# Half of the output gate's row in the differential mixer, gate transfers on GpSimd's queue, and seams in a new order, in a fused hybrid layer

## The chip, the cores and the metric

The kernel runs on one core of a Trainium2 chip. Five engines work beside each other, each with a queue of its own that it goes through in order: TensorE (PE in the profile, its weight loads PEld), VectorE (DVE), ScalarE (ACT), GpSimd (POOL) and SyncE (SP), which here only issues transfers. The metric is the device time of one execution in microseconds, the median of several runs.

## What is computed

One layer of a hybrid model on 512 positions of 2048 channels, and a norm behind it. All of it is fp32.

```python
mod = silu(c) @ w_ada + b_ada                     # 3 x 2048: shift, scale, gate
u = rms_norm(x, norm_w) * (1 + scale) + shift
proj = u @ w_in                                   # q, k, v, z of mixers A, B, C and the gates g_a, g_b, g_c
o_a = diff_attention(a_q, a_k, a_v, lam)          # 8 heads, two softmax maps each, one minus lam times the other
o_b = retention(b_q, b_k, b_v)                    # 8 heads, decaying scores, rotated q and k
o_c = dilated_mixture(c_q, c_k, c_v)              # 3 groups of 8 heads, windows of 1, 2 and 4 steps
y_m = (o_m * silu(m_z)) @ w_proj_m                # for m in a, b, c
merged = sigmoid(g_a) * y_a + sigmoid(g_b) * y_b + sigmoid(g_c) * y_c
h = x + gate * (merged @ w_out)
out = rms_norm(h, final_norm_w)
```

`gate`, the last third of `mod`, is a row of 2048 numbers (call it the output's gate; `gate phase` below means the merging of one mixer).

## The kernel before

Activations lie transposed, channels on the 128 partitions and the 512 positions along the free dimension. Every fp32 operand of a product is split into a high and a low part in a type that TensorE takes (`uh`, `ul` for the layer's input u; `wh`, `wl` for weights; `yh`, `yl` for a mixer's gated output), and `mm3` (L174) multiplies high by high, low by high and high by low into the same accumulator. A weight tile is loaded as `wr` by SyncE (1024 x 128, 512 KB), ScalarE casts it to `wh`, VectorE subtracts `wl`. There are three buffers of each. A projection of 128 columns takes two such tiles and 48 products. Accumulators are the eight banks of PSUM: two called `pj`, six called `at`. Nearly all instructions are recorded by one helper, so their line is L86 and they are told apart by their tiles.

The work goes in stages: projections in a form that saves products (up to some 1370 us, untouched by the change); mixer C; its gate phase; mixer A; its gate phase; mixer B; its gate phase; the output.

- **Mixer C** (the loop over heads behind L1073) keeps its order as written (`pinned`). A head makes its third key and z by four half projections (`half_step`, 24 products each), between which the scores of three groups stand. Queries and keys of the first two groups come from DRAM (`ql`, `kc`, `r`), `band` and `tri4` are masks.
- **Mixer A** (`a_scores`, `a_turn`, `a_values`, `rms_gate`): each of 8 heads projects Q, K and Z. In the middle of each projection (`mid`) the former head's leftover work is placed: transposing its scores e0 to e3, its values, its norm (square root on ScalarE, a reciprocal of 128 x 512 on VectorE), and then this head's scores.
- **Mixer B** (`rotate`, `b_scores`, `b_values`): four pairs of heads, Q and K rotated with `cos` and `sin`, two Z.
- **`gate_phase`** (L770) multiplies `y` by `w_proj` in 16 tiles (db), four or six of which start ahead of the mixer's last output. `gate_cols` loads the gate tile `gsg` (two buffers), `close` multiplies the accumulator by it, adds the sum so far (`gpr`, one buffer, from `part` in DRAM) and stores it back to `part` from ScalarE's queue. In the last phase the sum is split to `mh`, `ml`.
- **Output**: `merged @ w_out` in five column groups, `n`; four accumulators (one for each 128 positions), the products of a group going tile by tile (`t`, 24 products each). `gate_part` takes 256 rows and 512 columns of `w_ada`, weighs each row with `silu(c)` and sums them on VectorE into `gacc` (32 loads `gwa` of 512 KB in all, 64 operations), two parts in each tile of the first group and one in each after; `gate_sum` adds over the partitions by a product with ones. `residual` multiplies by the gate and adds to `hx`.

A scheduler places the instructions of mixers A and B, the gate phases and the output by a model of their durations and then keeps each engine's order; C and the stages ahead are pinned. So what a line in the source moves is seen only in the engines' order.

## Time and profile before

| what | us |
|---|---|
| median of 3 runs (2648.42 to 2651.3) | 2649.44 |
| the profiled execution | 2653.55 |
| its span, first to last instruction | 2651.8 |
| TensorE busy | 2543.9 |
| VectorE busy | 1919.4 |
| ScalarE busy | 1132.2 |
| GpSimd busy | 290.5 |

The profile shows one execution. Busy time counts an engine's instructions, a transfer's issue not among them. TensorE is busy for 96% of the span, so the seams between stages are read in a table of stretches: the width of a stretch less PE's busy time is what TensorE stood still, and the granted clock below 1.00 means that some of its products ran at 1.2 instead of 2.4 GHz. A wait is put down to what came last. The rows stand in a section of their own below.

### The profile page before, as it was taken

The page shows a single profiled execution, that of the slowest core. Times are in us where ns is not written, and L with a number is a line of the kernel's source. Part 1 is how long each engine was busy: PE and PEld are TensorE (multiplying, and loading weights), DVE is VectorE, ACT ScalarE, POOL GpSimd, SP SyncE. Part 2 cuts the span into 40 slices and gives each one's busy share as a digit, 9 for nine tenths or more (in the row PEclk, how much of TensorE's full clock was granted, in tenths as well). Part 3 has the DMA queues.
Part 4 walks back from the last instruction along what each step waited for, and adds up shares of the span by engine and source line. Part 5 has one row for each costly group of instructions (what it writes and reads, how often), then busy time and mean ns, then how long its engine had stood idle before and what let it go on. Part 6 is the DMA issues. An engine that isn't in the chain of part 4 may idle for free. (4 is left out here: it accounts for less than half of the span.)

```text
span 2651.8 us, 36979 instructions
## 1 busy us (share of the span) xinstructions
PE 2543.9 (96%) x14539; PEld 2231.4 (84%) x14539; DVE 1919.4 (72%) x2646; ACT 1132.2 (43%) x1461; POOL 290.5 (11%) x336
## 2 busy tenths in 40 slices
PE   6989999999999999999999999999999989999898
PEld 5777778999999999998878888788888768878678
DVE  7994888777787777877786776357767456776664
ACT  4224433443443333333336665346656145643122
POOL 2342001221122221212000000000000000000000
PEclk9999999999999999999999999999999999999999
DMA  9776666766666666676665554643233663337862
GB/s 343 253 272 227 233 206 232 235 209 204 225 221 220 225 216 214 220 232 220 222 200 152 159 149 133 191 124 88 83 93 87 189 183 106 89 106 216 303 210 104
DMA packets 386082, 503.26 MB, mean 190 GB/s; under 512 B 18898, under 2 KB 250084, under 8 KB 384756
## 3 DMA queue, kind: packets, MB, share of 16 engines
q1 hardware_dynamic: 364340, 448.83, 52.9%
q0 software_dynamic: 10048, 35.23, 3.8%
q10 hardware_dynamic: 11520, 16.85, 1.7%
q8 instruction: 114, 1.87, 0.3%
q14 instruction: 60, 0.49, 0.1%
HBM read 449.33 MB, written 51.51 MB: 189 GB/s over the span
## 5 line engine op out<-in xcount | busy, mean ns | idle before, releaser
L86 ACT CAST xh<-xr 128x2048 fp32r<-128x2048 f32 x196 | 374.2, 1909 | 584.7 <-PE at L86 494.3
L86 DVE TENSOR_TENSOR xl<-xr,xh 128x2048 fp32r<-128x2048 f32 x196 | 451.2, 2302 | 195.5 <-ACT xh L86 193.9
L86 ACT CAST wh<-wr 128x1024 fp32r<-128x1024 f32 (+2 forms) x275 | 240.2, 890 | 324.0 <-PE at L86 102.4
L86 PE MATMUL pj<-uh,wl 128*128 128x512 f32 x944 | 370.8, 393 | 5.9 <-DVE wl L86 3.3
L86 PE MATMUL pj<-uh,wh 128*128 128x512 f32 x944 | 373.6, 396 | 2.9 <-ACT wh L86 2.3
L86 PE MATMUL pj<-ul,wh 128*128 128x512 f32 x944 | 369.6, 392 | 0.0
L86 DVE TENSOR_TENSOR wl<-wr,wh 128x1024 fp32r<-128x1024 f32 (+2 forms) x241 | 240.9, 1013 | 142.2 <-ACT wh L86 141.3
L86 DVE TENSOR_TENSOR xr<-xr 128x512 f32<-128x512 f32 x448 | 329.1, 735 | 18.0 <-DMA xr<-in_w_in_dram 6.7
L86 PE MATMUL at<-fh,xl 128*128 128x256 f32 x864 | 246.2, 285 | 4.5 <-DVE xl L86 4.4
L86 PE MATMUL at<-fl,xh 128*128 128x256 f32 x864 | 245.3, 284 | 0.0
L86 PE MATMUL at<-fh,xh 128*128 128x256 f32 x864 | 245.2, 284 | 0.0
L86 PEld LDWEIGHTS pj<-uh,wl 128*128 128x128 f32 x944 | 178.1, 189 | 44.7 <-DVE wl L86 4.5
L86 PEld LDWEIGHTS pj<-uh,wh 128*128 128x128 f32 x944 | 178.6, 189 | 38.1 <-ACT wh L86 2.7
L86 PEld LDWEIGHTS pj<-ul,wh 128*128 128x128 f32 x944 | 178.6, 189 | 35.1
L86 PEld LDWEIGHTS at<-fh,xl 128*128 128x128 f32 x864 | 166.6, 193 | 5.9 <-DVE xl L86 5.5
L86 PEld LDWEIGHTS at<-fh,xh 128*128 128x128 f32 x864 | 166.6, 193 | 0.0
L86 PEld LDWEIGHTS at<-fl,xh 128*128 128x128 f32 x864 | 166.6, 193 | 0.0
L86 PE MATMUL at<-uh,xl 128*128 128x256 f32 x576 | 163.1, 283 | 0.0
L86 PE MATMUL at<-ul,xh 128*128 128x256 f32 x576 | 163.1, 283 | 0.0
L86 PE MATMUL at<-uh,xh 128*128 128x256 f32 x576 | 163.1, 283 | 0.0
L86 PE MATMUL at<-yh,wh 128*128 128x512 f32 x336 | 132.0, 393 | 6.4 <-DVE gsg L86 6.4
L86 PE MATMUL at<-yh,wl 128*128 128x512 f32 x336 | 131.4, 391 | 0.0
(378 smaller groups left out, 5713.7 us busy)
## 6 DMA issues: line engine op xcount, KB each, us to landing
xr<-in_w_in_dram SPq DMA_DIRECT2D x224, 512.0 KB, 4.6
xr<-in_w_in_dram SPq DMA_DIRECT2D x84, 1024.0 KB, 5.1
wr<-in_w_in_dram SPq DMA_DIRECT2D x116, 512.0 KB, 3.9
wa<-in_w_ada_dram SPq DMA_DIRECT2D x20, 1024.0 KB, 8.7
wr<-in_w_out_dram SPq DMA_DIRECT2D x32, 512.0 KB, 5.1
gwa<-in_w_ada_dram SPq DMA_DIRECT2D x32, 512.0 KB, 5.6
wr<-in_w_in_dram SPq DMA_DIRECT2D x32, 448.0 KB, 9.1
wb<-in_w_ada_dram SPq DMA_DIRECT2D x12, 1024.0 KB
```

Source lines behind the costliest of these rows:

```text
L86: return lambda *a, **k: pin(f(*a, **k))
```

## The change

- **Entry of mixer C**: the fourth weight load, `band` and `tri4` are issued behind the first queries and keys; the first head's scores stand behind the second half of its first projection.
- **Gate phases**: gate loads, part loads and part stores are issued by GpSimd. The tiles go in turn: three for gates in C (two `gsg`, one `gpr`); four gates and two parts in A (two of each from mixer A's pool, `gwa` and `gacc`); three gates in B (`gx` from the new pool).
- **The output's gate**: half of its row (two column groups of 512) is summed in mixer A, one part behind the splitting of K and one behind silu in each head. `gate_row(0)` in head 4 and `gate_row(1)` as the last thing left of mixer A add over the partitions and store 512 numbers to DRAM. The output loads them as `gsum` and sums the other half, one part a tile in groups 0 and 1, with the sum over partitions in the next group's second tile.
- **Mixer B**: v_load, the scores of pair 0 and the second head's values move: both heads' scores stand in the middle of the second Z, and values(1) ahead of the first head's norm.
- **Output**: gate, `gsum`, `finw`, `hx` and parts are loaded by GpSimd; odd groups take two `at` and two `pj`, the last group `at`.

```diff
@@ gate_phase
+        def turn_tile(kinds, db):
+            pool, tag, bufs = kinds[db % len(kinds)]
+            return (pool or fresh[0]).tile([P, S], F32, tag=tag, name=tag, bufs=bufs)
-            sgs[db] = gp.tile([P, S], F32, tag="gsg", name="gsg", bufs=2)
+            sgs[db] = turn_tile(gate_tiles, db)
-                sync.dma_start(out=sgs[db], in_=graw_dram[db])
+                nc.gpsimd.dma_start(out=sgs[db], in_=graw_dram[db])
-                sync.dma_start(out=sgs[db], in_=gate_of[g0][db])
+                nc.gpsimd.dma_start(out=sgs[db], in_=gate_of[g0][db])
-                pr = gp.tile([P, S], F32, tag="gpr", name="gpr", bufs=1)
-                sync.dma_start(out=pr, in_=part_dram[db])
+                pr = turn_tile(part_tiles, db)
+                nc.gpsimd.dma_start(out=pr, in_=part_dram[db])
-                nc.scalar.dma_start(out=part_dram[db], in_=sg)
+                nc.gpsimd.dma_start(out=part_dram[db], in_=sg)
@@ mixer C, entry
-    half_load(3)
     first = load_first_qk(0)
-    raw2, raw3 = (load_turned(2, 0), load_turned(3, 0)), None
+    raw2 = load_turned(2, 0), load_turned(3, 0)
+    half_load(3)
+    sync.dma_start(out=band, in_=k_band)
+    sync.dma_start(out=tri4, in_=k_tri4)
...
         half_step(4 * hd + 1, more)
+        if not prev:
+            h.first_scores(*first[0], first[1])
+            h.scores(1, *second[0], second[1])
+            late.extend([query, h.first_exps])
@@ mixer A
+    def gate_split(n):
+        acc = gacc.pop(n)
+        r, h, l = w_tiles([P, 512])
+        act.copy(h, acc)
+        dve.tensor_sub(l, acc, h.bitcast(F32))
+        return r, h, l
+    def gate_sum(h, l):
+        ps = at()
+        pe.matmul(ps, lhsT=ones_r, rhs=h, start=True, stop=False)
+        pe.matmul(ps, lhsT=ones_r, rhs=l, start=False, stop=True)
+        return ps
+    def gate_row(n):
+        r, h, l = gate_split(n)
+        ps = gate_sum(h, l)
+        act.copy(r[0:1, :], ps[0:1, :])
+        nc.gpsimd.dma_start(out=gate_dram[n:n + 1], in_=r[0:1, :])
...
+        with tc.issue_after(low_part):
+            if hd == 4:
+                gate_row(0)
+            gate_part(ap, hd // 4, hd % 4 * 2)
...
         sz = silu(ap, proj(A_Z + hd * P, mid=rest))
+        with tc.issue_after(last_silu[0]):
+            gate_part(ap, hd // 4, hd % 4 * 2 + 1)
...
+    def last_left(f=left[2]):
+        f()
+        gate_row(1)
@@ mixer B
+            if a == 1:
+                vpair += v_load(bp, 1, 2 * pr * P, "v")
+            for x in ((), (0, 1))[a] if pr == 0 else (a,):
+                b_scores(2 * pr + x, ks_[x], qs[x], pts[x])
...
-            gated(0)
             values(1)
+            gated(0)
@@ output
+    nc.gpsimd.dma_start(out=gsum, in_=gate_dram.rearrange("n c -> (n c)").partition_broadcast(P))
+    dve.tensor_add(gate[:, 0:1024], gate[:, 0:1024], gsum)
-        pss = [at() for _ in range(NT)]
+        pss = [(at if n % 2 == 0 or i < 2 else pj)() for i in range(NT)]
+            if parts_of and t == 1:
+                dve.tensor_add(gate[:, cs], gate[:, cs], gate_sum(*parts_of))
-            for _ in range(2 if n == 0 else 1):
-                gate_part()
+            if n < 2:
+                gate_part(fp, 2 + n, t)
```

Three places in the engines' order. **SyncE from the last head of mixer A to the start of mixer B.** The names are tiles and what they are loaded from; `in_w_proj_a` are the weights of gate phase A, `in_w_in` then those of mixer B. Before, from the load of `cos` on:

```order
L86 DMA cos<-in_k_cos_dram 128x512
L86 DMA sin<-in_k_sin_dram 32x512 x2
L86 DMA wr<-in_w_proj_a_dram 128x8x128
L86 DMA sin<-in_k_sin_dram 32x512 x2
L86 DMA dec<-in_k_decay_dram 128x512
L86 DMA wr<-in_w_proj_a_dram 128x8x128 x2
L86 DMA gpr<-part 128x512
L86 DMA gsg<-g_70 128x512
L86 DMA wr<-in_w_proj_a_dram 128x8x128
L86 DMA gpr<-part 128x512
L86 DMA wr<-in_w_proj_a_dram 128x8x128
L86 DMA gsg<-g_70 128x512
```

After, from the first weight of gate phase A to behind `cos`:

```order
L86 DMA wr<-in_w_proj_a_dram 128x8x128 x6
L86 DMA wr<-in_w_proj_a_dram 128x768
L86 DMA wr<-in_w_proj_a_dram 128x8x128 x10
L86 DMA wr<-in_w_in_dram 128x8x128 x6
L86 DMA cos<-in_k_cos_dram 128x512
L86 DMA sin<-in_k_sin_dram 32x512 x4
L86 DMA wr<-in_w_in_dram 128x8x128
L86 DMA dec<-in_k_decay_dram 128x512
```

The loads of gates and parts are gone from the queue, and `cos` and `sin` have moved from the front of the phase to behind six weight loads of mixer B.

**TensorE in head 4 of mixer A**, around the last scores (`k0h` to `k1l` are the split keys, `q` the two split queries, `pj<-uh` products of the projection of Z). Before, with 24 products of Z ahead of the first row:

```order
L86 MATMUL at<-sqs,ones_r 128x512
L86 MATMUL at<-k0h,q_16938 128x128
L86 MATMUL at<-k0l,q_16938 128x128
L86 MATMUL at<-k1h,q_16939 128x128
L86 MATMUL at<-k1l,q_16939 128x128
L86 MATMUL at<-k0h,q_16938 128x256
L86 MATMUL at<-k0l,q_16938 128x256
L86 MATMUL at<-k1h,q_16939 128x256
L86 MATMUL at<-k1l,q_16939 128x256
L86 MATMUL at<-k0h,q_16938 128x384
L86 MATMUL at<-k0l,q_16938 128x384
L86 MATMUL pj<-uh_112,wh 128x512
```

After, from the gate's second product with ones on; the first, the norm's and the smaller scores stand right behind K's last products, with nothing of Z between them:

```order
L86 MATMUL at<-wl,ones_r 128x512
L86 MATMUL at<-k1h,q_16973 128x384
L86 MATMUL at<-k1l,q_16973 128x384
L86 MATMUL at<-k0h,q_16972 128x512
L86 MATMUL at<-k0l,q_16972 128x512
L86 MATMUL at<-k1h,q_16973 128x512
L86 MATMUL at<-k1l,q_16973 128x512
L86 MATMUL at<-ident,e_17135 128x128
L86 MATMUL pj<-uh_105,wh 128x512
L86 MATMUL pj<-ul_121,wh 128x512
L86 MATMUL pj<-uh_105,wl 128x512
```

No product of Z stands ahead of the scores any more; the first comes behind the last score and the transposition of e0 (`at<-ident,e`).

**VectorE at the same place**, from the splitting of K's first half on. Before:

```order
L86 TENSOR_TENSOR k0l<-pj,k0h 64x512 x2
L86 TENSOR_TENSOR k1l<-pj,k1h 64x512 x2
L86 ISA e_17086,st<-at,cau 128x128
L86 ISA st 128x1
L86 TENSOR_TENSOR wl<-wr,wh 128x1024
```

After:

```order
L86 TENSOR_TENSOR k0l<-pj,k0h 64x512 x2
L86 ISA e_17135,st<-at,cau 128x128
L86 ISA st 128x1
L86 RECIPROCAL rs<-rs 128x512
L86 TENSOR_TENSOR k1l<-pj,k1h 64x512 x2
L86 TENSOR_TENSOR wl<-gacc,wh 128x512
L86 SCALAR_TENSOR_TENSOR rs<-at,daw,rs 128x512
L86 TENSOR_SCALAR gacc<-gwa,sc 128x512
L86 TENSOR_TENSOR rs<-rs,sz 128x512
L86 SCALAR_TENSOR_TENSOR gacc<-gwa,sc,gacc 128x512
```

The norm's reciprocal (`rs`) has moved ahead of `k1l`, and the gate's split (`wl<-gacc`) and first part stand among what follows; `wl<-wr`, the low half of Z's second weight tile before, now stands 27 rows behind the row of `k0l`.

## Rows read from the trace of the kernel before

**Rows 1.** The page, its first row of busy times (engine, busy us, share of the span, instructions), and of its second part the row of GB/s, one number for each fortieth of the span.

```profile
PE 2543.9 (96%) x14539; PEld 2231.4 (84%) x14539; DVE 1919.4 (72%) x2646; ACT 1132.2 (43%) x1461; POOL 290.5 (11%) x336
...
GB/s 343 253 272 227 233 206 232 235 209 204 225 221 220 225 216 214 220 232 220 222 200 152 159 149 133 191 124 88 83 93 87 189 183 106 89 106 216 303 210 104
```

**Rows 2.** Busy time by stretch; columns: from and to, width, busy us of PE, PEld, DVE, ACT and POOL with the number of instructions, mean granted TensorE clock (1.00 is 2.4 GHz), busy share of the DMA engines, GB/s. The stretches are: entry of mixer C, gate phase C, heads of mixer A, gate phase A, start of mixer B, pairs of B, gate phase B, output.

```profile
1373.00:1393.00 20.00, 14.75 (x61) 12.23 (x60) 14.69 (x33) 9.68 (x16) 2.15 (x3) 0.83 0.88 284
1630.00:1710.00 80.00, 77.05 (x356) 63.80 (x355) 32.34 (x40) 28.10 (x38) 1.86 (x2) 1.00 0.61 182
1710.00:2038.00 328.00, 325.24 (x1519) 269.40 (x1519) 222.74 (x436) 197.88 (x332) 0.00 (x0) 1.00 0.34 99
2038.00:2123.00 85.00, 80.81 (x355) 65.82 (x354) 39.50 (x51) 22.60 (x32) 0.00 (x0) 0.98 0.58 172
2123.00:2180.00 57.00, 46.82 (x189) 36.90 (x188) 30.99 (x55) 22.21 (x43) 0.00 (x0) 0.91 0.65 195
2180.00:2350.00 170.00, 166.15 (x767) 137.49 (x766) 123.87 (x195) 105.00 (x187) 0.00 (x0) 1.00 0.35 102
2350.00:2448.00 98.00, 95.14 (x416) 77.67 (x415) 64.66 (x78) 33.91 (x43) 0.00 (x0) 0.98 0.57 171
2448.00:2652.00 204.00, 181.22 (x956) 154.97 (x954) 121.96 (x175) 49.20 (x82) 0.00 (x0) 0.95 0.60 204
```

**Rows 3.** Timeline of PE, its last product.

```profile
2643.45 0.28 PE L86 MATMUL pj<-lh,ml 128*128 128x256 f32 x1
```

**Rows 4.** What PE waited for in the whole span: us in total, times, longest.

```profile
PE at L86 <- DVE gsg L86: 6.4, 4, 2.3
PE at L86 <- DVE res L86: 5.9, 1, 5.9
...
PE pj L86 <- ACT gh L86: 5.6, 1, 5.6
```

**Rows 5.** Timeline of PE at the entry of mixer C; columns: start us, duration us, engine, line, operation, out<-in, shapes, and in brackets the idle time before it and what ended it.

```profile
1383.22 0.33 PE L86 MATMUL at<-kc,qh 128*128 128x128 f32 x1 [4.41 <-ACT kc L86]
```

**Rows 6.** Timeline of SyncE's queue there (SPq), the same columns.

```profile
1373.40 0.34 SPq L86 DMA_DIRECT2D band<-in_k_band_dram  x1
...
1374.80 0.52 SPq L86 DMA_DIRECT2D ql<-qk  x1
```

**Rows 7.** Timeline of PE in head 4 of mixer A, behind the projection of K: the first and the last of 24 products of Z and the last of the scores that follow.

```profile
1901.30 0.39 PE L86 MATMUL pj<-uh,wh 128*128 128x512 f32 x1
...
1906.51 0.39 PE L86 MATMUL pj<-uh,wl 128*128 128x512 f32 x1
...
1910.65 0.39 PE L86 MATMUL at<-k1l,q 128*128 128x512 f32 x1
```

**Rows 8.** Timeline of VectorE at the output, the summing of the gate's parts.

```profile
2460.07 0.49 DVE L86 TENSOR_SCALAR gacc<-gwa,sc 128x512 f32<-128x512 f32 x1 [1.66 <-DMA gwa<-in_w_ada_dram]
...
2465.24 1.54 DVE L86 SCALAR_TENSOR_TENSOR gacc<-gwa,sc,gacc 128x512 f32<-128x512 f32 x2 [1.12 <-DMA gwa<-in_w_ada_dram]
```

**Rows 9.** Timeline of ScalarE in head 4 of mixer A, at the place of rows 7: the splitting of K and the norm of the head before.

```profile
1902.39 1.17 ACT L86 CAST k0h<-pj 64x512 fp32r<-64x512 f32 x2
...
1907.82 1.28 ACT L86 ACT_TABLE_LOAD   x1
1909.11 0.69 ACT L86 ACTIVATE rs<-at,eps 128x512 f32<-128x512 f32 x1
```

**Rows 10.** Timeline of VectorE at the same place.

```profile
1903.65 1.38 DVE L86 TENSOR_TENSOR k0l<-pj,k0h 64x512 fp32r<-64x512 f32 x2
1906.28 1.40 DVE L86 TENSOR_TENSOR k1l<-pj,k1h 64x512 fp32r<-64x512 f32 x2 [1.24 <-ACT k1h L86]
...
1907.93 1.22 DVE L86 TENSOR_TENSOR wl<-wr,wh 128x1024 fp32r<-128x1024 f32 x1
...
1909.96 3.35 DVE L86 RECIPROCAL rs<-rs 128x512 f32<-128x512 f32 x1
...
1914.15 0.68 DVE L86 TENSOR_TENSOR rs<-rs,sz 128x512 f32<-128x512 f32 x1
```

**Rows 11.** Timeline of PE at the start of mixer B, two of its waits.

```profile
2148.57 0.79 PE L86 MATMUL pj<-uh,wl 128*128 128x512 f32 x1 [2.78 <-DVE wl L86]
...
2171.70 1.02 PE L86 MATMUL at<-q,k0h 128*128 128x512 f32 x4 [3.94 <-ACT k0h L86]
```

**Rows 12.** Timeline of SyncE's queue at the start of mixer B.

```profile
2148.21 0.32 SPq L86 DMA_DIRECT2D gpr<-part  x1
...
2160.71 0.32 SPq L86 DMA_DIRECT2D gpr<-part  x1
```

**Rows 13.** The page's DMA issues: out<-in, queue, operation, count, KB each, median us from issue to landing.

```profile
gpr<-part SPq DMA_DIRECT2D x32, 256.0 KB, 3.9
...
gsg<-g SPq DMA_DIRECT2D x32, 256.0 KB, 3.0
...
wtb<-bounce POOLq DMA_DIRECT2D x8, 512.0 KB, 5.1
...
qk<-c POOLq DMA_DIRECT2D x5, 512.0 KB, 3.5
...
g<-z POOLq DMA_DIRECT2D x4, 512.0 KB, 8.5
```

**Rows 14.** Timeline of POOL, one issue of a DMA.

```profile
1377.43 0.71 POOL L659 DMA_DIRECT2D vd<-s  x1 [2.58 <-DVE s L86]
```

More of the change, by code (lines that the diff above doesn't have):

```diff
@@ L118, in hybrid_kernel @@
     qk_dram = [dram.tile([8, P, S], F32, tag=f"qk{i}", name=f"qk{i}") for i in range(len(QK))]
+    gate_dram = dram.tile([2, 512], F32, tag="gated", name="gated")
     br_dram = dram.tile([NF + NM, P, P], F32, tag="brd", name="brd")
@@ L803, in gate_phase @@
         if then is not None:
-            then()
+            fresh[0] = then()
         def close(db):
@@ L1093, in hybrid_kernel, with query @@
             prev.weigh(sz)
-        else:
-            h.first_scores(*first[0], first[1])
-            late.append(h.first_exps)
-        h.scores(1, *second[0], second[1])
+            h.scores(1, *second[0], second[1])
         def more():
             third[:] = query_tiles(), key_tiles()
-            if hd < 7:
+            if 0 < hd < 7:
                 got["first"] = load_first_qk(hd + 1)
-        late.append(lambda: split_query(got["raw3"], third[0]))
+        def query():
+            split_query(got["raw3"], third[0])
+        if prev:
+            late.append(query)
         half_step(4 * hd + 1, more)
+        if not prev:
+            h.first_scores(*first[0], first[1])
+            h.scores(1, *second[0], second[1])
+            late.extend([query, h.first_exps])
         split_keys(half_ps[0], third[1])
@@ L1114, in hybrid_kernel, with more @@
             late.append(lambda: split_first_qk(*got["first"]))
-        half_step(4 * hd + 2, lambda: got.update(vs=load_values(hd)))
+        def more():
+            got["vs"] = load_values(hd)
+            if not prev:
+                got["first"] = load_first_qk(1)
+        half_step(4 * hd + 2, more)
         if not prev:
@@ L1149, in hybrid_kernel @@
     gate_bias()
-    gate_phase(G_C, w_pc, "first", left=left)
+    gate_phase(G_C, w_pc, "first", [(gp, "gsg", 2), (gp, "gsg", 2), (gp, "gpr", 1)], left=left)
     c_es.close()
@@ L1221, in a_values, with gate_part @@
         return o, rms_squares(ap, o)
+    gacc = {}
+    def gate_part(pool, n, jq):
+        if jq == 0:
+            gacc[n] = pool.tile([P, 512], F32, tag="gacc", name="gacc")
+        acc = gacc[n]
+        wa = pool.tile([P, 2, 512], F32, tag="gwa", name="gwa", bufs=2)
+        nc.gpsimd.dma_start(out=wa, in_=w_ada[0, jq * 256:(jq + 1) * 256, 2 * D + n * 512:2 * D + (n + 1) * 512]
+                            .rearrange("(j p) c -> p j c", p=P))
+        for j in range(2):
+            k = jq * 2 + j
+            if k == 0:
+                dve.tensor_scalar_mul(acc, wa[:, j, :], sc[:, 0:1])
+            else:
+                dve.scalar_tensor_tensor(out=acc, in0=wa[:, j, :], scalar=sc[:, k:k + 1],
+                                         in1=acc, op0=ALU.mult, op1=ALU.add)
+    def gate_split(n):
[14 more added lines that the diff above has]
+        nc.gpsimd.dma_start(out=gate_dram[n:n + 1], in_=r[0:1, :])
     left = [None, None, None]
@@ L1260, in hybrid_kernel @@
         sz = silu(ap, proj(A_Z + hd * P, mid=rest))
+        with tc.issue_after(last_silu[0]):
+            gate_part(ap, hd // 4, hd % 4 * 2 + 1)
         left = [lambda es=es, pth=pth, ptl=ptl: a_turn(es, pth, ptl), values,
                 lambda hd=hd, got=got, sz=sz: rms_gate(ap, *got, daw, sz, hd)]
-    gate_phase(G_A, w_pa, "mid", left=left)
+    def last_left(f=left[2]):
+        f()
+        gate_row(1)
+    gate_phase(G_A, w_pa, "mid", [(gp, "gsg", 2), (ap, "gwa", 2)], [(gp, "gpr", 1), (ap, "gacc", 1)],
+               left=left[:2] + [last_left])
     a_es.close()
@@ L1344, in second @@
         def second(values=values, gated=gated):
+            values(1)
             gated(0)
-            values(1)
         left = [lambda f=values: f(0), second, lambda f=gated: f(1)]
@@ L1357, in merged_open @@
             ml.append(mp.tile([P, S], F32R, tag=f"ml{i}", name=f"ml{i}"))
-    gate_phase(G_B, w_pb, "last", mh, ml, left=left[1:], then=merged_open)
+        return mp
+    gate_phase(G_B, w_pb, "last", [(gp, "gsg", 2), (gp, "gsg", 2), (None, "gx", 1)], [(gp, "gpr", 1)], mh, ml,
+               left=left[1:], then=merged_open)
     g_es.close()
@@ L1378, in hybrid_kernel @@
     gate = fp.tile([P, D], F32, tag="gate", name="gate")
+    gsum = fp.tile([P, 1024], F32, tag="gsum", name="gsum")
     finw = fp.tile([P, D], F32, tag="finw", name="finw")
@@ L1430, in residual @@
             dve.tensor_mul(hx[i][:, cs], hx[i][:, cs], finw[:, cs])
-    sync.dma_start(out=gate, in_=b_ada[0, 2 * D:3 * D].partition_broadcast(P))
-    sync.dma_start(out=finw, in_=fin_w.partition_broadcast(P))
+    nc.gpsimd.dma_start(out=gate, in_=b_ada[0, 2 * D:3 * D].partition_broadcast(P))
+    nc.gpsimd.dma_start(out=gsum, in_=gate_dram.rearrange("n c -> (n c)").partition_broadcast(P))
+    dve.tensor_add(gate[:, 0:1024], gate[:, 0:1024], gsum)
+    nc.gpsimd.dma_start(out=finw, in_=fin_w.partition_broadcast(P))
+    parts_of = None
     for n in range(LAST):
@@ L1443, in hybrid_kernel @@
                 i = t // 2
[L1444 removed]
+                nc.gpsimd.dma_start(out=hx[i], in_=x[0, i * P:(i + 1) * P, :])
+            if parts_of and t == 1:
+                cs = slice((n + 1) * 512, (n + 2) * 512)
+                dve.tensor_add(gate[:, cs], gate[:, cs], gate_sum(*parts_of))
+                parts_of = None
             for j in range(nk):
```

55 lines of the change are left out of this document (10 added, 45 removed).

## The prediction, made before the changed kernel ran

> **What bounds the kernel now.** The page's busy row comes first: TensorE is busy 2543.9 us of a span of 2651.8 [rows 1]. Everything else has room, so only two things can be won or lost: time in which TensorE has no operand, and time in which it multiplies at the lower of its two clock levels (1.2 instead of 2.4 GHz). The table of stretches gives both for the places that the diff touches [rows 2]: width less PE busy is idle time, and since the granted clock is at one level or the other, a mean of 0.91 over 57 us means 0.18 x 57 = 10.3 us at the lower level, of which half is lost. So per stretch (idle + clock): entry of the dilated mixer 5.2 + 3.4 = 8.7; gate phase C 2.9; heads of mixer A 2.8 in 328 us; gate phase A 4.2 + 1.7 = 5.9; start of mixer B 10.2 + 5.1 = 15.3; pairs of B 3.9; gate phase B 2.9 + 2.0 = 4.8; output 22.8 + 10.2, of which some 8 idle and part of the clock are the tail behind the last products [rows 3], so 20. Sum 64 us: no seam can give more than its row. Then the waits of PE by tile [rows 4], and the timelines of the seams for what stood ahead of the late operand.
>
> **The change part by part**, each against the profiled execution's 2653.55 us.
>
> *Entry of mixer C.* TensorE waits 4.41 us for the first keys [rows 5]; SyncE issues band and mask at 1373.40 and the first query only at 1374.80 [rows 6]. Now query and keys go first (1.4 us earlier), and the second half of the first projection, whose weights are already there, is multiplied ahead of the scores: 24 products at (1906.51 - 1901.30) / 23 = 0.2265 us are 5.44 us [rows 7]. Cover of 6.8 us against a wait of 4.4: the wait goes, and with it the lower clock behind it. What is late next is the splitting of the third pair of tiles, which has the same 5.4 us. **-8** (-6.5 to -8.7).
>
> *Gate phase C.* One wait of PE for a gate tile, most of 2.9 us. Three tiles in turn instead of two, and no issue on ACT ahead of its casts: **-2.4** (-2.9 to +3, if POOL's loads are slow, see the first rival).
>
> *Heads of mixer A.* Sixteen loads of 512 KB go on POOL's queue and 32 operations on VectorE (the first of each sum 0.49 us, the others 0.77) [rows 8]: a pair of 1.5 us behind the splitting of K and one behind silu in each head. The first stands ahead of score operations, the second ahead of a wl of the next query. Eight heads lose 2.8 us in all now [rows 2], so their slack is unknown from below: nothing is lost if each pair fits in it, 2 us a head if one pair and a bit falls on the path. I take 1 us in the six heads that have no gate row behind them: **+6** (0 to +14).
>
> *Head 4, gate_row(0).* This is the largest loss. Before, 24 products of Z (5.4 us) stand ahead of the scores, and wl for the other 24 is made among them. The order of the changed kernel has all 48 products of Z behind the gate's sum, all scores and the transposition of e0, and on VectorE the reciprocal and the gate's operations ahead of k1l. Counted from the end of K: on ACT k0h 1.17, table load 1.28, square root 0.69 [rows 9], so the reciprocal begins at 3.1 and takes 3.35 (6.5); k1l 1.40 (7.9); gate wl 0.7, two products of rs 0.7 each, gacc 0.49 and 0.77 (11.2); then the second map's e0 at 11.5; yl 0.7, vl and wl of Z 1.22 each, and nine small ones worth some 3.4 together (18) [rows 8, 10]. TensorE's work in that time is what ran from 1906.73 to 1910.88 before without the three products of Z among it, 3.5 us, and three short ones of the gate, some 4 in all [rows 7]. Idle some 14 us; behind idle stretches of that kind the stretches of [rows 2] lose 1.7 to 5.1 us to the lower clock, so 2 more, less 0.4, a head's share of today's idle time: **+15** (+5, if the scheduler's wait for k1l is shorter than added up, to +19).
>
> *Entry of gate phase A, gate_row(1).* The last head's reciprocal, rs twice and wl now follow sqs in a row: wait for the square root 2.3 (0.3 + 1.28 + 0.69), 3.35, 1.4, 1.22 are 8.3 us from sqs to the operand of the fourth product, against 1.4 us of products. Before, that wl stood ahead of the reciprocal. 6.9 and a little clock: **+7.5** (+3 to +9).
>
> *Gate phase A.* Four gate tiles, two part tiles, loads and stores all on POOL's queue, in whose order they stand as the gates come. PE's waits for gsg are 6.4 us in the run [rows 4], and most of the 4.2 idle here is that. **-5** (-5.9 to +2).
>
> *Start of mixer B.* SyncE carries gate and part loads in line with B's weights: parts are still loaded at 2148.21 and, the last, at 2160.71, when TensorE has long been in B [rows 11, 12]; the DVE adds that wait for them stand ahead of wl. PE then waits 2.78 for wl and 3.94 for k0h [rows 11]. With SyncE holding only weights, VectorE done with the gates, and 72 products instead of 24 between K's projection and the first score, K's rotation has 16.3 us of cover instead of 5.4. Cos and sin then wait for mixer A's memory to come free with POOL's last stores; they land near the time they are needed: **-13.5** (-15.3 to -6).
>
> *Pairs of B, and B to its gate phase.* values(1) ahead of the first norm covers the wait for the first head's squares, which comes once a pair and is most of 3.9 us: **-3** (-3.9 to +1). The late products moved behind db 2 to 4 cover the wait for yh there, most of 2.9 us, and the clock behind it [rows 2]: **-3.5** (-4.8, the upper end is the first rival's).
>
> *Output.* PE waits 5.9 for the residual that frees its accumulators and 5.6 for gh [rows 4], each with the lower clock behind it. With accumulators alternating, the first goes; with half of the parts done in mixer A, 8 loads instead of 16 in the first column group and the sum put off by a group, so does the second. What stays is the change from group 0 to 1: wl stands behind four residual operations, some 2 us. 14.5 MB (gate 1, gsum 0.5, finw 1, parts 4, hx 4, weights 4) in 43.5 us is 333 GB/s, near the best slice of the page, 343 [rows 1]; but VectorE waits for parts only where wl has 8 us of slack. **-17** (-20 to -3).
>
> Sum: -8 - 2.4 + 6 + 15 + 7.5 - 5 - 13.5 - 3 - 3.5 - 17 = -23.9; 2653.55 - 23.9 = 2629.6. The median of the runs lies 4.1 us under the profiled execution: **2625.4**.
>
> **A rule weighed.** Loads of 512 KB issued by POOL land in 3.5 to 5.1 us here, in one group 8.5, those of 256 KB by SyncE in 3.0 to 3.9 [rows 13]; a POOL issue takes 0.71 [rows 14]. The Trainium skill, SBUF — State Buffer, in its note on the "DVE blocks DMA" trap, says that descriptors of GpSimd's transfers can't be written while VectorE runs a two-port operation, such as an fp32 copy, and advises the other queues. That speaks against moving plain loads here. By that note each moved load would land later by what is left of such an operation, of which gacc's first, 0.49 us [rows 8], may be one, so that the sum would be worse by up to 0.5 us for each load that something waits for; no run so far shows it, and the sum above holds none. What lateness of these loads would do is the first rival.
>
> **The rivals.**
>
> *POOL's loads are late (slower).* In gate phase B there is one part tile: add 0.7, issue 0.71, landing L, add. TensorE takes 5.44 us a gate, so L above 4.0 stretches the phase, VectorE's adds for late parts standing ahead of wl. At L = 6.2 it is 2.2 us for 14 gates less one gate of slack, 25 us; the parts of the output would come late in the same way and 14 of its 17 go. -23.9 + 39 is 15 above: 2664 by the median. It decides from L about 5.1, where both prices reach 24. For it: the one group at 8.5, and stores in the same queue. Against it: 256 KB is half of the loads that took 3.5 to 5.1.
>
> *The gate rows cost a third.* If what stands behind K in head 4, and at the entry of gate phase A, finds TensorE with more work than I count, the 28.5 us of losses are 10: 2607. For it: only 2.8 us are idle in the heads now. Against it: the order is fixed, and the operations have known durations.
>
> *Each seam has a second wait just behind the first.* Rotation at B's start, wl at the output's groups, the splitting at C's entry: half of the 52.4 us comes, 26 against 28.5: 2652, no change. Against it: idle time in small pieces, as in the heads of A, leaves the clock at 1.00 [rows 2], so a seam with half a wait keeps less than half of its loss. That only the gate part moves and no seam is covered is excluded by the order.
>
> **How the numbers follow.** Forecast (2610 to 2642) 0.58; gate rows cheap 0.17; second waits 0.10; POOL late 0.15. About 5 us (0.2%) is what a measurement of this kernel tells from no change. The second waits fall within that or just outside: faster 0.77, same 0.08, slower 0.15. The range reaches down to gate rows at a third with B's start and the output in full, 2602, and up to the second waits, 2655.
>
> **What would show it.** In the profile after: no wait for kc, gsg, gh or res above 1 us; at head 4 a hole of TensorE of some 14 us with the lower clock behind it, waiting for k1l and wl; one of 6 to 7 us ahead of gate phase A's fourth tile, on wl; B's start without waits above 1 us. Wrong if PE waits for gpr's adds in gate phase B, if gacc stands ahead of wl in PE's waits at the output, or if head 4 has no hole.

## The result and the profile after

| | us |
|---|---|
| changed kernel, median of 4 runs (2635.07 to 2637.19) | 2636.29 |
| kernel before, median of 4 runs on the same chip (2648.42 to 2651.3) | 2649.53 |
| ratio, with its 95% interval | 0.9949 [0.9932, 0.9966] |
| the profiled execution after (its span) | 2637.08 (2635.3) |

The change makes the kernel 13.2 us faster. The two profiled executions differ by 16.5, since that of before lies 4.0 above its median and that of after 0.8. The page of after answers to [rows 1]: TensorE's busy time hasn't changed, so the gain is time in which it stood still, 107.9 us before (2651.8 - 2543.9) and 91.6 after. Time at the lower clock level isn't less: the mean granted clock is 0.987 in both executions.

```profile
PE 2543.7 (97%) x14539; PEld 2232.4 (85%) x14539; DVE 1911.6 (73%) x2645; ACT 1132.5 (43%) x1462; POOL 382.3 (15%) x489
```

GpSimd's row grows by 153 instructions and 91.8 us because, other than is said above of busy time, it does count the issues of its transfers: all 19 instructions of POOL in mixer A below are such issues.

To see where, each stage is bounded by starts of products in TensorE's own timeline: mixer C from the last product of the projections ahead of it, a gate phase from its first product of `y`, mixers A and B from the last one of the gate phase before, the output from its first product of `mh`. Lengths in us:

| stage | before | after | difference | predicted |
|---|---|---|---|---|
| ahead of mixer C (not touched) | 1372.98 | 1374.82 | +1.8 | 0 |
| mixer C | 254.87 | 251.26 | -3.6 | -8 |
| gate phase C | 94.66 | 91.94 | -2.7 | -2.4 |
| mixer A | 310.93 | 327.48 | +16.6 | +21 |
| gate phase A | 96.84 | 102.72 | +5.9 | +2.5 |
| mixer B | 220.31 | 202.65 | -17.7 | -16.5 |
| gate phase B | 94.38 | 89.69 | -4.7 | -3.5 |
| output, with the tail | 206.82 | 194.73 | -12.1 | -17 |
| sum | 2651.79 | 2635.29 | -16.5 | -23.9 |

The view of [rows 2] on the stages of after, with the same columns:

```profile
1374.82:1626.08 251.26, 245.08 (x1329) 209.93 (x1327) 188.73 (x448) 162.22 (x309) 23.84 (x26) 0.99 0.55 157
1626.08:1718.02 91.94, 91.54 (x422) 75.97 (x421) 37.08 (x49) 35.01 (x52) 19.59 (x34) 1.00 0.70 209
1718.02:2045.50 327.48, 314.96 (x1446) 258.58 (x1444) 229.14 (x448) 186.98 (x321) 12.86 (x19) 0.98 0.38 109
2045.50:2148.22 102.72, 95.37 (x409) 76.69 (x408) 55.07 (x82) 30.89 (x46) 22.18 (x42) 0.97 0.60 183
2148.22:2350.87 202.65, 201.37 (x924) 166.95 (x923) 145.22 (x233) 125.89 (x222) 3.53 (x7) 1.00 0.42 124
2350.87:2440.56 89.69, 89.69 (x399) 74.09 (x398) 59.02 (x71) 31.79 (x40) 15.58 (x29) 1.00 0.59 174
2440.56:2635.29 194.73, 180.45 (x965) 155.76 (x963) 102.55 (x145) 49.75 (x82) 15.86 (x24) 0.96 0.51 180
```

Three stages have almost no idle time left: gate phase C, mixer B and gate phase B are within 1.3 us of PE's busy time, at full clock. Mixer A, gate phase A and the output have 12.5, 7.4 and 14.3 us of idle time, and they are also the ones with a clock below 0.99. What PE waits for in the whole span, as in [rows 4], names the operands:

```profile
PE at L86 <- ACT wh L86: 6.9, 3, 4.9
...
PE at L86 <- DVE k1l L86: 4.8, 8, 2.4
PE at L86 <- DVE wl L86: 4.8, 3, 3.2
...
PE at L86 <- DVE e L86: 2.7, 2, 2.3
...
PE at L86 <- DVE gsg L86: 0.5, 1, 0.5
```

The waits of [rows 4] are gone (`gsg` 0.5 instead of 6.4; `res` and `gh` no longer stand in the list). Their successors are read from the timelines, where a time "lost" is the distance between the starts of products less what the same products take with neither a wait nor the lower clock; it is good to about half a us. A "hole" is a stretch in which TensorE has no product to run.

**Head 4 of mixer A** loses 14.4 us (0.9 before). PE there, from the gate's first product with ones on:

```profile
1898.15 0.39 PE L86 MATMUL at<-wh,ones_r 128*128 128x512 f32 x1
...
1902.77 0.33 PE L86 MATMUL at<-k1h,q 128*128 128x128 f32 x1 [1.46 <-ACT k1h L86]
...
1906.40 0.80 PE L86 MATMUL at<-k1l,q 128*128 128x128 f32 x2 [2.41 <-DVE k1l L86]
...
1913.31 0.47 PE L86 MATMUL at<-ident,e 128*128 128x128 f32 x1 [2.32 <-DVE e L86]
```

The idle time comes in six pieces between 1898 and 1915, 8.4 us together; the rest goes to the lower clock level, at which TensorE stood for 13.7 us there. And VectorE in the same stretch, which answers to [rows 10]: the reciprocal now stands ahead of `k1l`, and the weight's `wl` comes only at 1913.71.

```profile
1901.57 3.35 DVE L86 RECIPROCAL rs<-rs 128x512 f32<-128x512 f32 x1
1904.95 1.40 DVE L86 TENSOR_TENSOR k1l<-pj,k1h 64x512 fp32r<-64x512 f32 x2
1906.38 0.69 DVE L86 TENSOR_TENSOR wl<-gacc,wh 128x512 fp32r<-128x512 f32 x1
...
1913.71 1.22 DVE L86 TENSOR_TENSOR wl<-wr,wh 128x1024 fp32r<-128x1024 f32 x1
```

**Entry of gate phase A** loses 11.0 us (0.7 before): 2.3 at the transposition ahead of it, and 8.8 behind the square sum `sqs`, in these rows of PE:

```profile
2064.48 0.39 PE L86 MATMUL at<-sqs,ones_r 128*128 128x512 f32 x1
...
2067.06 0.50 PE L86 MATMUL at<-yh,wh 128*128 128x512 f32 x1 [1.72 <-ACT wh L86]
...
2071.76 0.79 PE L86 MATMUL at<-yh,wl 128*128 128x512 f32 x1 [3.25 <-DVE wl L86]
```

VectorE gives the reason: that `wl` has the reciprocal and both products of `rs` ahead of it.

```profile
2065.63 3.35 DVE L86 RECIPROCAL rs<-rs 128x512 f32<-128x512 f32 x1 [1.79 <-ACT rs L86]
...
2070.49 2.35 DVE L86 TENSOR_TENSOR wl<-wr,wh 128x1024 fp32r<-128x1024 f32 x2
```

**The output, from column group 0 to 1**, loses 9.7 us. PE waits for a weight's high part:

```profile
2489.18 1.22 PE L86 MATMUL at<-wh,mh 128*128 128x512 f32 x2 [4.94 <-ACT wh L86]
```

ScalarE has been idle for 18.55 us at that moment. The cast of the weight stands behind the cast of the gate's sum in its order, and that one waits for `gacc`:

```profile
2487.57 0.62 ACT L86 CAST wh<-gacc 128x512 fp32r<-128x512 f32 x1 [18.55 <-DVE gacc L86]
2488.09 1.99 ACT L86 CAST wh<-wr 128x1024 fp32r<-128x1024 f32 x2
```

VectorE in turn has nothing to do but to wait for the last loads of the gate's parts:

```profile
2485.92 1.54 DVE L86 SCALAR_TENSOR_TENSOR gacc<-gwa,sc,gacc 128x512 f32<-128x512 f32 x2 [2.98 <-DMA gwa<-in_w_ada_dram]
```

So a load sets a product of another weight, by way of two engines that work in order.

**Mixer C.** The 8.8 us lost at its entry are down to 0.3, but 4.3 new ones are lost from 1408 to 1423: PE waits for the next pair of keys and then runs 3.4 us at the lower level. (The 77 products from 1408.02 on take 15.57 us, the same 77 of a later head, without a wait, 11.31.)

```profile
1411.17 0.39 PE L86 MATMUL at<-kc,qh 128*128 128x256 f32 x1 [2.11 <-DVE kc L86]
```

The splitting of that pair begins on ScalarE at 1407.88, though the last of its loads had landed at 1390.24. Ahead of it in ScalarE's order stands the issue of a store, that of `wt`, a result of the first head's softmax, which VectorE finishes at 1407.36:

```profile
1407.18 0.18 DVE L86 RECIPROCAL wt<-wt 128x4 f32<-128x4 f32 x1
...
1407.43 0.40 ACTq L86 DMA_DIRECT2D bounce<-wt  x1
1407.88 1.15 ACT L86 ACTIVATE qh<-r 128x512 fp32r<-128x512 f32 x1 [1.12 <-issue]
```

By these rows it is the same pattern as in the output: something that waits for VectorE stands in ScalarE's order ahead of an operand that TensorE needs. No run moved that store.

### The profile page after: what moved, and what is told of

Its sections match the earlier page's. It is cut to its first block, busy times and chain, and to the rows that moved or that the text cites. A ratio compares the mean times of both kernels' runs of the same rounds, so it can differ in the third digit from the quotient of the medians.

```text
span 2635.3 us, 36994 instructions
## 1 busy us (share of the span) xinstructions
PE 2543.7 (97%) x14539; PEld 2232.4 (85%) x14539; DVE 1911.6 (73%) x2645; ACT 1132.5 (43%) x1462; POOL 382.3 (15%) x489
```

## The experiments

All ratios are against the kernel before on the chip of that run; the changed kernel's own is 0.9949. Edits are diffs against the changed kernel, with `...` where lines are left out. The stages ahead of mixer C, which no edit touches, take 1369.0 to 1374.8 us in the profiled executions of all these kernels, so a difference of some 5 us between two whole kernels says little by itself, and the stages that an edit touches say more.

### Where the gate's sum over the partitions stands

The theory: head 4 and the entry of gate phase A lose time only because `gate_row` stands ahead of operands that TensorE needs sooner. The rival: its chain (cast, subtraction, two products with ones) costs the same wherever it is put.

```diff
@@ e1: mixer A, behind the splitting of K, and behind silu
-            if hd == 4:
-                gate_row(0)
...
+            if hd == 3:
+                gate_row(0)
```

> The changed kernel with gate_row(0) taken from behind the splitting of K in head 4 and put behind the last part of the row's first half, after silu of head 3. Theory (place): the hole of TensorE in head 4 comes from the row standing between K's split and the scores, so that no product of Z covers the norm's reciprocal; in the order of this kernel 24 products of Z stand ahead of the scores again. Head 4 then loses about 1.3 us like its neighbours instead of 14.4, and nothing comes in head 3: 13 us less, 2623 us. Rival (work): VectorE has too much to do in head 4 with the row's split and a new sum; then the loss moves with the row or stays above 6 us, and the kernel is at 2630 or more.

Measured: 2632.5, ratio 0.9924 [0.9909, 0.9939]. Head 4 has no hole any more (1.3 us lost, as in other heads). But PE's products with ones now stop it behind head 3's Z, ahead of the transposition of its scores:

```profile
1875.28 0.80 PE L86 MATMUL at<-wh,ones_r 128*128 128x512 f32 x1 [5.32 <-ACT wh L86]
```

The sum of the last parts stands on VectorE behind the end of silu, `sz`, and its cast on ScalarE behind it:

```profile
1872.07 0.68 DVE L86 TENSOR_TENSOR sz<-pj,gsg 128x512 f32<-128x512 f32 x1
1872.67 1.53 DVE L86 SCALAR_TENSOR_TENSOR gacc<-gwa,sc,gacc 128x512 f32<-128x512 f32 x2
```

In all 11.2 us are lost there (5.5 in the wait, 5.7 behind it, with 10.2 us at 1.2 GHz), against 14.4 in head 4. By the trace some 2 us are won (11.2 + 1.3 against 14.4; mixer A is 2.7 shorter), by the ratio up to 6.6 (0.0025 x 2650), with intervals that overlap; 3.0 us of the profiled difference lie ahead of mixer C, where nothing was edited. The place moves the loss and takes little of it away.

The same for the second row, moved behind the last part in head 7:

```diff
@@ e2: mixer A
+            if hd == 7:
+                gate_row(1)
...
-    def last_left(f=left[2]):
-        f()
-        gate_row(1)
```

> The changed kernel with gate_row(1) put behind the last part, after silu of head 7, instead of behind the last norm. Theory (place): the 11 us lost at the entry of gate phase A come from wl of the phase's third or fourth tile standing behind reciprocal and norm, because the row holds one of three weight buffers across the norm; moved ahead, the weights' wl stand ahead of the reciprocal and 9 to 10 us go: 2626 us. Rival (work): the reciprocal of 3.35 us and the wait for the square root are on TensorE's path in any case, and less than 4 us go.

Measured: 2637.53, ratio 0.9946 [0.993, 0.9963]: no gain. The 8.8 us behind `sqs` are gone and the same wait has come ahead of the last head's transposition and values, with 5.5 us lost in it and 6.3 behind:

```profile
2049.62 0.79 PE L86 MATMUL at<-wh,ones_r 128*128 128x512 f32 x1 [5.32 <-ACT wh L86]
```

Two places for each row, and neither is free. In the two new ones TensorE's order has the product with ones where the chain that feeds it, from the last sum of parts by way of ScalarE, isn't done yet.

### The output's group change

```diff
@@ e3: output
+            if parts_of is not None and t == 0:
+                parts_of = gate_split(parts_of)[1:]
...
-            parts_of = gate_split(2 + n)[1:]
+            parts_of = 2 + n
```

This puts the cast of the gate's sum behind the cast of the next group's first weight.

> The changed kernel with the split of the output gate's half row (cast of gacc and its low part) behind the cast of the next column group's first weight tile instead of ahead of it. Theory (ScalarE's order): TensorE's wait of 4.9 us from group 0 to 1 is the weight cast standing behind the cast of gacc, which waits for the last part's load; with the weight cast first the wait and the lower clock behind it go, 6 to 8 us: 2629 us. Rival (VectorE's order): wl of that tile stands behind four residual operations and the last parts, and TensorE waits for wl nearly as long; less than 3 us go.

Measured: 2633.0, ratio 0.9928 [0.9913, 0.9943]. The wait for ScalarE's `wh` is gone, so the reading of its order above is right. What is late next is VectorE's `wl`, behind the residual's operations, and 7.0 of the 9.7 us stay lost:

```profile
2489.92 0.47 PE L86 MATMUL at<-wh,ones_r 128*128 128x512 f32 x1 [1.05 <-DVE res L86]
...
2493.42 0.80 PE L86 MATMUL at<-wl,mh 128*128 128x512 f32 x1 [2.56 <-DVE wl L86]
```

All three edits together:

> All three moves in one kernel. If the three holes are independent, the gains add: 13 + 9 + 7 = 29, so 2607 us. If VectorE's or ScalarE's work is the limit and the holes only move, it is above 2620.

Measured: 2632.73, ratio 0.9925 [0.9909, 0.9942], no better than e1 or e3 alone. Both waits of 5.5 us are there, and the output loses 8.7.

### The entry of mixer C

```diff
@@ e5: mixer C, loads and first head as in the kernel before
+    half_load(3)
     heads = [c_head(hd) for hd in range(8)]
     first = load_first_qk(0)
...
-    half_load(3)
...
+            h.first_scores(*first[0], first[1])
+            late.append(h.first_exps)
+        h.scores(1, *second[0], second[1])
...
         half_step(4 * hd + 1, more)
-        if not prev:
-            h.first_scores(*first[0], first[1])
-            h.scores(1, *second[0], second[1])
...
```

> The changed kernel with the entry of mixer C as before: loads in the old order and the first head's scores ahead of the second half projection. Theory: the entry won about 9 us, but 5 of them are given back in the same mixer, at the first head's end, where the keys of the next head are late now; so undoing it costs 3 to 4 us: 2640 us, with TensorE waiting for kc at the entry and not 30 us later. Rival: the later wait is there in any case and the entry is worth its 8 to 9: 2645 us.

Measured: 2635.89, ratio 0.9958 [0.9943, 0.9972]. The waits of the first keys are back, 8.2 us lost with them, while the 4.3 us at 1408 are gone. Mixer C is 253.5 long, 2.2 more than in the changed kernel; 0.0009 of the ratio (2.4 us) agrees with that, though the intervals overlap. In all twelve kernels with the new entry mixer C takes 249.2 to 251.8 us, in the two with the old one 253.5 and 254.9. The new entry isn't worth the 8 us of its wait, because its second wait comes with it.

### The start of mixer B: queue, tiles, or order

Of the 15.0 us lost here 14.4 came back; 0.6 stays. Three things changed at once: the queue of the gate phases' transfers, the number of tiles in turn, and mixer B's own order. Each was undone alone.

```diff
@@ e4: the queue alone, in gate_phase
-                nc.gpsimd.dma_start(out=sgs[db], in_=gate_of[g0][db])
+                sync.dma_start(out=sgs[db], in_=gate_of[g0][db])
...
-                nc.gpsimd.dma_start(out=pr, in_=part_dram[db])
+                sync.dma_start(out=pr, in_=part_dram[db])
...
-                nc.gpsimd.dma_start(out=part_dram[db], in_=sg)
+                nc.scalar.dma_start(out=part_dram[db], in_=sg)
```

> The changed kernel with the transfers of the three gate phases back on SyncE (gate and part loads) and ScalarE (part stores), the tiles in turn as they are. Theory (queue): the 13.5 us won at the start of mixer B come from SyncE being free of loads that wait for gates; with them back the gates lag again and 6 to 13 us of B's start return: 2642 to 2649 us. Rival (buffers): four gate tiles and two part tiles let the loads run ahead, the gates end with TensorE's products, and the queue is indifferent: 2634 to 2638 us.

Measured: 2628.16, ratio 0.994 [0.9921, 0.9959], the same as on GpSimd's queue. Mixer B's start loses nothing. The DMA issues of the changed kernel (out<-in, queue, operation, count, KB each, median us to landing):

```profile
gpr<-part POOLq DMA_DIRECT2D x24, 256.0 KB, 3.5
...
gsg<-g POOLq DMA_DIRECT2D x19, 256.0 KB, 3.9
...
gwa<-g POOLq DMA_DIRECT2D x8, 256.0 KB, 4.3
gacc<-part POOLq DMA_DIRECT2D x8, 256.0 KB, 5.0
```

and of e4, the same transfers:

```profile
gpr<-part SPq DMA_DIRECT2D x24, 256.0 KB, 2.8
...
gsg<-g SPq DMA_DIRECT2D x19, 256.0 KB, 4.6
...
gwa<-g SPq DMA_DIRECT2D x8, 256.0 KB, 2.7
gacc<-part SPq DMA_DIRECT2D x8, 256.0 KB, 4.7
```

Three are sooner by SyncE and one later, and the time doesn't change.

```diff
@@ e8: the tiles alone, one line for each phase (A's shown)
-    gate_phase(G_A, w_pa, "mid", [(gp, "gsg", 2), (ap, "gwa", 2)], [(gp, "gpr", 1), (ap, "gacc", 1)],
+    gate_phase(G_A, w_pa, "mid", [(gp, "gsg", 2)], [(gp, "gpr", 1)],
```

> The changed kernel with the tiles of the three gate phases as before (two for gates, one for parts), the transfers on GpSimd's queue as they are. Theory (tiles): the run with the transfers on SyncE kept all of the gain, so the tiles in turn carry it; with two and one the gates lag behind TensorE in gate phase A, VectorE has their operations in B's start, and 8 to 14 us come back in phases C and A and B's start: 2645 us in the scale of the first result. Rival (order of B): the projections ahead of the first scores carry B's start, and under 5 us come back, those in the phases.

Measured: 2651.73, ratio 1.0012 [1.0, 1.0025]. All of the change's gain is gone. Mixer B's start loses 9.2 us, gate phase A behind its entry 4.2 (1.8 in the changed kernel), and gate phases C and B are 1.3 and 2.9 longer. PE at B's start:

```profile
2179.84 0.80 PE L86 MATMUL pj<-uh,wh 128*128 128x512 f32 x1 [5.15 <-DVE rf L86]
```

The rotation that PE waits for stands on VectorE behind gate operations, and these behind loads:

```profile
2174.78 0.69 DVE L86 TENSOR_TENSOR gsg<-at,gsg 128x512 f32<-128x512 f32 x1 [4.42 <-DMA gsg<-g]
...
2178.49 0.69 DVE L86 TENSOR_TENSOR gsg<-at,gsg 128x512 f32<-128x512 f32 x1
2179.10 0.68 DVE L86 TENSOR_TENSOR rf<-pj,cos 128x512 f32<-128x512 f32 x1
```

A gate's load waits there for the store of the tile that it reuses, as POOL's timeline of e8 shows:

```profile
2157.17 0.54 POOL L802 DMA_DIRECT2D gsg<-g  x1 [1.64 <-DMA part<-gsg]
```

With two tiles VectorE does its last gate operation at 2182.78; with four, in the changed kernel, at 2155.60:

```profile
2155.60 0.68 DVE L86 TENSOR_TENSOR gwa<-gwa,gacc 128x512 f32<-128x512 f32 x1
```

```diff
@@ e9: mixer B's order alone
+        vpair = v_load(bp, 1, 2 * pr * P, "v")
...
-            for x in ((), (0, 1))[a] if pr == 0 else (a,):
-                b_scores(2 * pr + x, ks_[x], qs[x], pts[x])
+            b_scores(2 * pr + a, ks_[a], qs[a], pts[a])
...
-            values(1)
             gated(0)
+            values(1)
```

> The changed kernel with mixer B in the order of before (v_load ahead of Z, each head's scores in the middle of its own Z, the first head's norm ahead of the second's values). Theory (tiles): B's start keeps its gain but for 1 to 3 us, and each of the three later pairs loses 1 us more, the wait for the squares: 2641 us. Rival (order of B): TensorE waits for wl, the rotation and k0h at B's start again, 6 us or more there: 2645 us or more.

Measured: 2648.65, ratio 1.0001 [0.9989, 1.0012]. The start of B loses 2.5 us instead of 0.6, each later pair 1.9 instead of 0.9, and the entry of gate phase B 7.3 instead of nothing:

```profile
2369.35 0.73 PE L86 MATMUL pj<-yh,wh 128*128 128x512 f32 x2 [2.22 <-ACT yh L86]
```

Together 1.9 + 3.0 + 7.3 = 12.2 us, and later tiles of gate phase B lose some 3 more, waiting for `wl`; the ratio gives 0.0052 x 2648 = 13.8. So B's order is worth about as much to the kernel as the tiles are, but at other places than B's start.

```diff
@@ e11: e4's queue and e8's tiles; mixer B's new order stays
```

> The changed kernel with the gate phases as before altogether: old tiles, SyncE and ScalarE, and mixer B in its new order. Theory (tiles): as with old tiles on GpSimd's queue, 8 to 14 us come back, and if SyncE's being held by loads that wait for gates adds to it, more than there: 2645 to 2650 us. Rival (order of B): B's start keeps 10 of its 13.5 us although SyncE and VectorE carry the lagging gates: 2640 us.

Measured: 2648.49, ratio 1.0001 [0.999, 1.0012], as e8. With the gate phases of the kernel before, and only B's order new, the start of B loses 10.8 us and gate phase A 6.5. So at this seam the tiles in turn carry most (the loss is 9 to 11 us without them), B's order 2, and the queue nothing that can be measured.

The output's 12.1 us were not taken apart in this way. That the accumulators in alternation took away the wait for `res`, and the fewer parts and the later sum that for `gh`, is read from the traces of before and after; no run undoes either alone.

### A version without the two holes

The sum over the partitions needn't be made in mixer A. Storing `gacc` itself (256 KB for each column group) and summing it at the output takes the chain out of heads 4 and 7, and with it both products with ones:

```diff
@@ e6: mixer A, and the output
-    def gate_row(n):
-        r, h, l = gate_split(n)
-        ps = gate_sum(h, l)
-        act.copy(r[0:1, :], ps[0:1, :])
-        nc.gpsimd.dma_start(out=gate_dram[n:n + 1], in_=r[0:1, :])
+    def gate_store(n):
+        nc.gpsimd.dma_start(out=gate_dram[n], in_=gacc.pop(n))
...
+            if n == 0 and t in (2, 4):
+                parts_of = gate_split((t - 2) // 2)[1:]
```

> The changed kernel without gate rows in mixer A: the sum of each half over 8 parts (128 x 512) is stored to DRAM as it is, loaded at the output, and split and added over partitions there, in tiles 2 to 5 of group 0. No product, cast or weight buffer for it in mixer A. Theory (place): both holes go, 13 in head 4 and 10 at the entry of gate phase A, and the output keeps its 10: 2613 us. Rival (work): VectorE's 32 operations of parts in the heads are what costs, and 10 us or more of the two holes stay: 2623 or more.

Measured: 2613.79, ratio 0.988 [0.986, 0.9901]. Both holes are gone, and the output loses 6.0 us at the group change instead of 9.7.

The second version also spreads the other 16 parts over tiles 1 to 6 of groups 0 and 1 and tiles 1 to 4 of group 2, with each sum in the middle of a group:

```diff
@@ e7: output, against e6
+    parts_of, done, splits = None, 0, [(0, 2), (0, 4), (1, 3), (2, 5)]
...
+            if (n < 2 and 0 < t < 7 or n == 2 and 0 < t < 5):
+                gate_part(fp, 2 + done // 8, done % 8)
+                done += 1
```

> As the kernel before this one, and the 16 parts that stay in the output are spread over tiles 1 to 6 of groups 0 and 1 and 1 to 4 of group 2, and each sum is split in the middle of a group, so that no cast of gacc stands between two groups. Theory: the wait for the weight cast from group 0 to 1 and most of the lower clock behind it go, 6 to 8 us more: 2606 us. Rival: residual operations on VectorE keep TensorE waiting at the change of groups, and it gains under 3 us on the kernel before it.

Measured: 2605.44, ratio 0.985 [0.9826, 0.9874]. Mixer A, gate phase A and the output of e7 in the view by stretch, against the third, fourth and seventh row of after above:

```profile
1712.47:2028.10 315.63, 310.21 (x1444) 256.31 (x1443) 228.46 (x447) 186.75 (x319) 12.88 (x19) 1.00 0.39 115
2028.10:2122.45 94.35, 91.59 (x408) 74.31 (x406) 51.78 (x75) 30.00 (x44) 21.41 (x40) 1.00 0.63 197
...
2416.03:2602.89 186.86, 177.75 (x969) 154.31 (x967) 103.73 (x148) 51.02 (x84) 16.42 (x25) 0.99 0.53 188
```

They are 11.9, 8.4 and 7.9 us shorter, all of it idle time and time at the lower level; the mean granted clock of the whole kernel rises from 0.987 to 0.995. With e4's queue in e7:

> The kernel with stored sums and spread parts, its gate phases' transfers on SyncE and ScalarE. If SyncE's loads land a little sooner and ScalarE's casts don't wait for them, B's start loses its last 2.8 us: 2602 us. If ScalarE's queue is held by the stores again, casts come late in the gate phases: 2608 us or more.

Measured: 2602.77, ratio 0.9828 [0.9807, 0.985], the fastest of all; next to e7 the intervals overlap. Either beats both kernels, by 40 to 46 us against before where the change as written wins 13.

## Why the prediction was right, and where its terms were not

The direction, the mechanisms of the gain (but for the queue's part at mixer B's start) and the two holes that pay for it came as forecast, and 2636.3 lies within the forecast's own range (2610 to 2642, narrower than the outer ends of 2602 and 2655 that it works out), 10.9 above its value. Of these, 5.6 are the errors of the terms (-18.3 in the touched stages instead of -23.9), 1.8 an untouched stretch, and 3.5 in the main the profiled execution's distance to the median, which was taken over from before as 4.1 and came to 0.8. The 5.6 are small by luck in part: the stages with too good a forecast (mixer C, the output, gate phase A) missed by 12.7 together, the others made up for 7.1 of that.

- **Head 4** (+15): +13.5. The order of VectorE was read rightly, reciprocal and gate ahead of `k1l` and `wl`, and Z's `wl` let TensorE go on 16.8 us behind K's last product, where 18 were added up. But the parts of the term came otherwise: not one hole of some 14 us but six waits of 8.4 together, of which `k1l` has 2.41 and `wl` 0.35 and the others are for `k0h`, `k0l`, `k1h` and `e`; and some 6 us by the lower clock instead of 2. That the two errors nearly cancel is luck, as far as the forecast goes.
- **Heads of mixer A** (+6): +3.1, what mixer A's +16.6 leave beside head 4. Each of the others loses 0.45 us more; the pairs of gate operations nearly fit. e7, which has the parts in the heads and no hole, has a mixer A that is 4.7 longer than before.
- **Entry of gate phase A** (+7.5): +10.3. From `sqs` to the operand the chain took 7.3 us, where 8.3 were added up, and TensorE waited 5.2 in it (1.72 and 0.22 for `wh`, 3.25 for `wl`) instead of 6.9; with the lower clock behind it, put at "a little", it came to 8.8. The transposition ahead of it wasn't counted.
- **Gate phases C and A** (-2.4, -5): -2.7, and -4.4, what gate phase A's +5.9 leave beside its entry.
- **Start of mixer B** (-13.5): -14.4, but not for the reason that "SyncE holding only weights" gives, so that it came so near is luck in part. That part of the step fell: with the transfers back on SyncE and ScalarE (e4) the start of B loses nothing. "VectorE done with the gates" holds, and it is the tiles that bring it (e8), with B's longer cover a smaller part (e9).
- **Pairs of B, and B to its gate phase** (-3, -3.5): -3.2 and -4.7; e9 takes both back.
- **Entry of mixer C** (-8): -3.6. The step that failed is the sizing of what is late next: the prediction named the splitting of the following tiles and took its cover of 5.4 us for enough. PE waited 2.11 us for such a `kc`, the next head's, and lost 4.3 with the lower clock. What held ScalarE until 1407.88, where that splitting begins, was by its rows the store of `wt`, which the prediction didn't look at.
- **Output** (-17): -12.1. The step that failed is "VectorE waits for parts only where wl has 8 us of slack". It looked at VectorE alone. The gate's sum goes through ScalarE too, whose cast of it stands ahead of the next group's weight; so the last part's load (`gwa` from `w_ada`, 5.0 us in the median of 32) stops `wh`. e3 moved that cast and the wait went; the wait for `wl`, which the prediction had put at some 2 us, then came to 2.56.

The signs that it named. No wait for `gsg`, `gh` or `res` above 1 us, and none of that size at B's start: so it is. No wait for `kc` above 1 us: one of 2.11 came, 28 us later than the old one. The hole of some 14 us in head 4 and that of 6 to 7 ahead of gate phase A's fourth tile came in pieces, as told. Of the signs of being wrong, `gacc` ahead of `wl` at the output came nearly: it stood ahead of `wh`, on ScalarE.

The rivals. *POOL's loads late* didn't come: `gpr` lands in 3.5 us, under the 5.1 from which it decides, and gate phase B is as wide as PE's busy time in it. *The gate rows cost a third* is excluded: heads, head 4 and gate phase A's entry cost 26.9 against the 28.5 counted. *Each seam has a second wait* came at two of the seams, C's entry and the output, not at B; these two terms fell short by 4.4 and 4.9.

The rule that was weighed, the note on the "DVE blocks DMA" trap in the Trainium skill, SBUF — State Buffer, changes nothing here that a run shows: e4, which follows its advice in the gate phases, has the same ratio (0.9940 against 0.9949, with intervals that overlap), and one of four groups of loads lands later by SyncE than by POOL. Whether some descriptors were held up can't be seen in the profile.

## What to carry to other kernels

When an operation is put into another engine's order, follow its whole chain through every engine that works in order: here the output's gate sum stopped a weight's cast on ScalarE, and a product with ones stopped TensorE wherever it was put. Better than a better place was here to cut the chain: store the sum as it is, and finish it where its result is needed and other products can stand in between. And before a transfer is moved to another queue, count the tiles in turn: at mixer B's start a third and fourth tile gave what the queue was given credit for.

## What the runs showed of the hardware

The same idle time can cost very different times at the lower clock. Behind a wait of 5.32 us in e1 TensorE's granted clock was 0.50 for 10.2 us, behind 4.94 at the output of the changed kernel for 10.2 too; behind 5.15 us in e8 it was 0.50 for 6.8, and behind 2.11 us in mixer C for 3.4. In head 4, where six waits of 0.4 to 2.4 us follow one another, it was 13.7. So a hole of some 5 us cost 8 to 12 us in all (8 in e8, 9.7 at the output, 11.2 in e1, 11.8 in e2, with the small waits behind it), and two holes of a kind needn't cost the same.

Nor does a lower clock always cost time. In e10 the same place of mixer C has a wait of 2.26 us, and the granted clock stays at 1.00 behind it:

```profile
1407.37 0.38 PE L86 MATMUL at<-kc,qh 128*128 128x256 f32 x1 [2.26 <-DVE kc L86]
...
1415.45 0.39 PE L86 MATMUL at<-p,vh 128*128 128x256 f32 x1 [1.30 <-DVE p L86]
```

Yet the 77 products take 15.75 us there and 15.57 in the changed kernel: at full clock TensorE comes sooner to the next operand, `p`, and waits for it.
